# A decoder layer with retrieved experts: 160 instead of 128 tokens take gathered rows, sums run over eight expert tiles, and the spill is spread

## The chip, the cores and the metric

The kernel runs on one core of one Trainium2 chip. A core has a matrix engine (TensorE, here PE), three engines for elementwise work (VectorE or DVE, ScalarE or ACT, GpSimd or POOL), a queue engine (SyncE, SP) and 16 DMA engines that move data between the chip's memory (HBM), the 128-partition working memory (SBUF) and back. PE writes into the accumulators (PSUM). The metric is device time in microseconds (us); lower is better. A time is the median of several executions; one execution is recorded by the hardware profiler.

## The reference

One inference step of one decoder layer, in float32, for 512 prompt tokens and 8 sample tokens (520 together, 2048 wide). Two attention branches are gated, multiplied by `w_out` and added to the input; this gives `h`. Then follows a mixer with retrieved experts (PEER). Of 16384 experts, each token takes 128: 8 heads choose 16 each by product keys. Cut to what matters:

```
hn = rmsnorm(h, norm2_w)                        # 520 x 2048
q = (hn @ wq) per head, in two halves
s = q . subkeys                                 # 8 heads x 2 halves x 128 keys
half_s, half_i = top_k(s, 16)
best_s, best_c = top_k(sums of pairs, 16)       # 16 of 256 candidates per head
experts = i1 * 128 + i2                         # 128 expert numbers per token
gates = softmax(best_s)
act = gelu(hn . u[experts])                     # 128 dot products of 2048 per token
y = h + sum over experts of gates * act * v[experts]
```

`u` and `v` have 16384 rows of 2048 numbers each.

## The kernel before

**Two ways for the experts.** The first `ND` = 392 tokens ("dense") are computed with all 16384 experts: PE multiplies every u row with every dense token, in 128 tiles of 128 experts; the result goes through gelu, is multiplied by a gate that is zero for experts not chosen, and PE multiplies this by all v rows. The last `NS` = 128 tokens ("gathered", one per partition) fetch only their chosen rows: an indirect DMA on POOL's queue brings, for one choice, one row of u or v for each of 128 tokens (128 x 2048 floats, 1 MB).

**Matmuls.** Every float32 weight is split into two parts, `wh` (rounded, ScalarE, L297) and `wl` (the rest, DVE, L299), and every product is three matmuls: wh by yh, wh by yl, wl by yh. `terms` (L331) issues them all on L336; a matmul has 128 columns of weights and as many moving columns as there are tokens. Weights are streamed in the order of `_plan`, 1 MB at a time, in two halves of 1024 columns; `wh` and `wl` have `WB` = 3 buffers of one half each. `terms` counts its columns and calls `tick` after every 16 x 260 of them.

**Stages.**
1. Projection and attention (78 tiles of `win`, matmuls of 260 columns, two per weight tile for the 520 tokens), then the branch products and `w_out`, also 260 and 260.
2. `wq` products, one per head (`q_product`): 392 and 128 columns.
3. u tiles 0 to 69 (`spill_u`): 48 matmuls of 392 columns, gelu, and the result goes out to HBM (`act_d`, issued by POOL). Under these tiles the routing runs: `halves_top` and `best_all` are generators, `tick` makes one step of one of them. `best_all` goes through the five token tiles of `TILES` (tile 0 holds the gathered tokens): top-16 searches on DVE, and for each half of the keys an equality mask on DVE (L1043), a product with the indices on POOL (L1045, 128 x 2048) and a sum on DVE (L1048). For tile 0 the expert numbers and gates go to `eg`. Then `build_g` makes the gates of the dense tokens as a matrix in HBM (`g_d`): for each four tokens DVE builds two masks (eA L1097, Bt L1099), POOL and ScalarE scale them (L1101, L1103, L1104), and PE multiplies them (L1080, 8 matmuls of 128 columns).
4. Experts, from about 2249 us: 32 groups of `GRP` = 4 expert tiles. `c_of` fetches a spilled result (L1232), or computes a u tile from tile 70 on, multiplies it by the gates (L1218) and splits it (L1220, L1221). `v_group` multiplies 4 tiles by v, 16 output chunks, and DVE adds each pair of chunks to `acc` (L1263).
5. `gathered` runs beside stage 4, as one more generator: 128 times a u row is fetched (L1155) and its dot product with `hn` taken on DVE (L1185, the row buffer is overwritten), then gelu and gates, then 128 v rows, each scaled and added to a sum on DVE (L1197). A row is due every `PACE` = 3.1 ticks; there are three row buffers. Before the last group the rest is drained, PE transposes the sum, and it is added to `acc`.

**Order.** PE's and SP's instructions run in the order in which the program writes them; from stage 4 on POOL's do too. The order of the others is set by a planner.

## Time and profile before

| | |
|---|---|
| median of 3 runs | 3904.21 us (3903.19 to 3906.29) |
| the profiled execution | 3891.22 us |
| its span | 3889.5 us |
| PE busy | 3812.2 us (98%), 25080 matmuls |
| PE weight loads (PEld) | 3779.9 us (97%) |
| DVE busy | 2753.0 us (71%) |
| ACT busy | 1436.4 us (37%) |
| POOL busy | 930.5 us (24%) |
| HBM read and written | 836.48 and 150.95 MB, 254 GB/s over the span |

An engine is busy while an instruction of it runs; matmuls overlap, so a busy PE is not PE at its full pace. The page of the profile divides the span into 40 slices and gives the busy share of each in tenths. In the views by line, `L299` is line 299, `wl<-wr,wh` names output and inputs, `x744` the number of instructions. A wait is put down to the instruction that ended it.

### The profile page before, as it was taken

The numbers are of one execution on the slowest core, as the hardware profiler recorded it, in microseconds if no ns is written. First come the engines' busy times: TensorE is split into PE (matmuls) and PEld (weight loads), VectorE is DVE, ScalarE is ACT, GpSimd is POOL, SyncE is SP. The second block draws the span as 40 slices with busy tenths as digits, with TensorE's granted clock in tenths as the row PEclk, the third lists the DMA queues.
The fourth block names the chain that finished last, engine by engine and source line by source line (L and its number), as shares of the span: only waits on it lengthen the run. The fifth ranks groups of instructions, "written<-read, shape, count | busy, mean of one in ns | idle before, by whom it ended". The sixth has DMA issues, their size and how long they took to land.

```text
span 3889.5 us, 61269 instructions
## 1 busy us (share of the span) xinstructions
PE 3812.2 (98%) x25080; PEld 3779.9 (97%) x25080; DVE 2753.0 (71%) x3925; ACT 1436.4 (37%) x2032; POOL 930.5 (24%) x944
## 2 busy tenths in 40 slices
PE   8999999999999999989999999999999999999999
PEld 8999999999999999989999999999999999999999
DVE  5444333778654357898666579999988888888864
ACT  5655444222322322323777532222222323232232
POOL 2111111223210000133666322222222222222200
PEclk9999999999999999999999999999999999999999
DMA  4233334667656333545544579898888889888853
GB/s 164 103 113 137 141 133 183 222 242 260 228 202 236 141 132 116 191 162 197 199 187 184 201 297 336 319 332 318 333 329 330 318 329 337 331 312 304 331 209 131
DMA packets 140761, 901.37 MB, mean 232 GB/s; under 512 B 20096, under 2 KB 21088, under 8 KB 56512
## 3 DMA queue, kind: packets, MB, share of 16 engines
q1 hardware_dynamic: 59296, 489.74, 33.5%
q0 software_dynamic: 66064, 380.27, 26.4%
q10 hardware_dynamic: 15120, 27.43, 2.2%
q8 instruction: 198, 3.24, 0.3%
q14 instruction: 83, 0.68, 0.1%
HBM read 836.48 MB, written 150.95 MB: 254 GB/s over the span
## 4 chain that ended last, share of the span: by engine, by line
PE 84%; DVE 8%; issue 4%; DMA 2%; ACT 1%; POOL 0%; ACTq 0%; POOLq 0%; DVEq 0%
PE mm L336 71%; PE vv L336 8%; DVE wl L299 3%; PE gq L1080 2%; DVE gb L1185 1%; DMA k<-q_d 1%; PE sc L976 0%; ACT wh L297 0%; DMA wr<-in_win 0%; PE a L510 0%; DVE acc L1263 0%; PE a L517 0%; DVE s1b L1048 0%; PE a L523 0%; DVE c L1221 0%
## 5 line engine op out<-in xcount | busy, mean ns | idle before, releaser
L297 ACT ACTIVATE wh<-wr 128x1024 fp32r<-128x1024 f32 x744 | 787.4, 1059 | 1840.3 <-PE mm L336 1454.3
L299 DVE TENSOR_TENSOR wl<-wr,wh 128x1024 fp32r<-128x1024 f32 x744 | 948.3, 1279 | 335.8 <-ACT wh L297 334.0
L336 PE MATMUL mm<-HH,wl 128*128 128x392 f32 x2176 | 755.1, 347 | 15.3 <-DVE wl L299 15.3
L336 PE MATMUL mm<-HH,wh 128*128 128x392 f32 x2176 | 759.1, 349 | 2.1 <-ACT wh L297 1.2
L336 PE MATMUL mm<-HL,wh 128*128 128x392 f32 x2176 | 756.0, 347 | 0.0
L336 PE MATMUL mm<-c,wh 128*128 128x392 f32 x2316 | 608.5, 343 | 3.9 <-DVE c L1221 3.9
L336 PE MATMUL mm<-S,wh 128*128 128x260 f32 x3048 | 589.0, 285 | 8.2 <-ACT S L380 8.2
L336 PE MATMUL mm<-S,wl 128*128 128x260 f32 x2664 | 545.0, 286 | 5.3 <-DVE wl L299 5.3
L336 PEld LDWEIGHTS mm<-S,wh 128*128 128x128 f32 x3048 | 460.2, 190 | 10.4 <-ACT S L380 8.2
L336 PEld LDWEIGHTS mm<-c,wh 128*128 128x128 f32 x2316 | 426.1, 189 | 6.9 <-DVE c L1221 6.1
L336 PEld LDWEIGHTS mm<-HH,wl 128*128 128x128 f32 x2176 | 412.2, 189 | 19.3 <-DVE wl L299 18.6
L336 PEld LDWEIGHTS mm<-S,wl 128*128 128x128 f32 x2664 | 414.5, 190 | 8.8 <-DVE wl L299 5.7
L336 PEld LDWEIGHTS mm<-HH,wh 128*128 128x128 f32 x2176 | 411.5, 189 | 4.0 <-ACT wh L297 1.5
L336 PEld LDWEIGHTS mm<-HL,wh 128*128 128x128 f32 x2176 | 411.6, 189 | 0.9
L336 PE MATMUL mm<-c,wl 128*128 128x392 f32 x1158 | 396.0, 342 | 1.4 <-DVE wl L299 1.4
L336 PE MATMUL mm<-S1a,wh 128*128 128x260 f32 x1520 | 311.0, 286 | 4.2 <-DVE S1a L381 4.1
L336 PE MATMUL mm<-S1b,wh 128*128 128x260 f32 x1520 | 312.2, 287 | 2.1 <-DVE S1b L381 2.1
L336 PE MATMUL vv<-c,wh 128*128 128x392 f32 x1108 | 293.0, 344 | 8.7 <-DVE c L1221 5.5
L1197 DVE SCALAR_TENSOR_TENSOR hb<-gb,dots,hb 128x2048 f32<-128x2048 f32 x127 | 298.1, 2347 | 4.4 <-DMA gb<-in_vn,idx 4.3
L1185 DVE SCALAR_TENSOR_TENSOR gb<-gb,hb 128x2048 f32<-128x2048 f32 x128 | 292.6, 2286 | 3.1 <-DMA gb<-in_un,idx 3.1
L1155 POOL DMA_INDIRECT gb<-in_vn,idx x128 | 158.7, 1240 | 462.5 <-DVE hb L1197 397.3
L336 PEld LDWEIGHTS mm<-S1a,wh 128*128 128x128 f32 x1520 | 235.0, 189 | 6.2 <-DVE S1a L381 5.1
(317 smaller groups left out, 5584.8 us busy)
## 6 DMA issues: line engine op xcount, KB each, us to landing
wr<-in_uT SPq DMA_DIRECT2D x128, 1024.0 KB, 4.9
wr<-in_v SPq DMA_DIRECT2D x128, 1024.0 KB, 7.3
wr<-in_win SPq DMA_DIRECT2D x78, 1024.0 KB, 4.8
g_d<-stg POOLq DMA_DIRECT2D x14, 1792.0 KB, 6.9
ga<-g_d POOLq DMA_DIRECT2D x32, 784.0 KB, 10.8
wr<-in_wout SPq DMA_DIRECT2D x16, 1024.0 KB, 4.8
out_s<-in_c SPq DMA_DIRECT2D x16, 1020.0 KB, 7.3
act_d<-t POOLq DMA_DIRECT2D x70, 196.0 KB, 2.6
```

What stands on the lines that cost most here:

```text
L297: A.activation(h, r, AF.Copy)
L299: V.tensor_tensor(l, r, h, op=OP.subtract)
L336: PE.matmul(ps, u, y[lo >= ND][:, lo % ND:hi - lo + lo % ND] if isinstance(y, tuple) else y[:, lo:hi], start=(begin and i == 0 and a == 0) ...
L1080: PE.matmul(ps[:, t], Bt[:, t], AA[:, t, x], start=x == 0, stop=x == 1)
L1155: G_.indirect_dma_start(out=g, out_offset=None, in_=src, in_offset=bass.IndirectOffsetOnAxis(ap=idx[:, j:j + 1], axis=0))
L1185: V.scalar_tensor_tensor(g, g, 1.0, hn, op0=OP.mult, op1=OP.mult, accum_out=dots[:, j:j + 1])
L1197: V.scalar_tensor_tensor(sums, g, coef[:, j:j + 1], sums, op0=OP.mult, op1=OP.add)
```

## The change

- Dense tokens: 360 instead of 392; gathered: 160 instead of 128. All dense matmuls have 360 columns; `wq` and `w_out` products have 360 and 160 (`w_out` had 260 and 260). The 160 gathered tokens come in two sets: 128 tokens with 128 rows each of u and v as before, and 32 tokens whose 128 choices are spread over four groups of 32 partitions (`RB` = 4), so that 32 fetches each of u and v do.
- `gathered` starts as soon as tile 0 of the routing is done, not in stage 4, and has a clock of its own in `tick`. Its pace in ticks depends on the stage: 4.0 in the rest of the routing, 3.5 in `build_g`, then 2.3 for u rows and 2.9 for v rows. From then on POOL's instructions run in written order.
- The dot products of u rows: in the routing all on POOL (product) and ScalarE (sum), in `build_g` all on DVE, in stage 4 every second one on POOL and ScalarE.
- Groups have 8 expert tiles (16 groups): one weight tile of v holds 8 x 256 columns for two output chunks, and `acc` gets half as many additions. Of every group 3 tiles are computed in place (positions 0, 3, 6) and 5 come from the spill: 80 are spilled instead of 70.
- Gathered tokens have their own part of the sum (`accg`, kept in HBM as `h_d`) and go out on their own. Their `hn` is made early by `hn_rows`, in the `wq` stage.
- `build_g` has 90 steps instead of 98, with three sets of masks instead of two, its gate products two steps behind instead of one, and 1.5 ticks per step instead of 1.33. Spill stores are issued three ticks later (`post`). Copies of cache rows are issued every 7 ticks instead of 9. Buffers are cut differently, so that they fit.

The diff, cut to its core:

```diff
-ND, NS = 392, 128
+ND, NS = 360, 160
+NA_, NB_, RB = 128, 32, 4
 TT, NTT = 128, 5
-TILES = [(ND, NS)] + [(i * (ND // 4), ND // 4) for i in range(4)]
-GC, NGC = 28, 14
-KA = 12
+TILES = [(ND + NB_, NA_), (ND, NB_)] + [(i * (ND // 3), ND // 3) for i in range(3)]
+GC, NGC = 24, 15
+KA = 11
 NEXP = 128
-NSPILL = 70
-GRP = 4
+GRP = 8
+GL = 4
+INLINE = {g * GRP + i for g in range(NEXP // GRP) for i in (0, 3, 6)}
+SPILLED = [i for i in range(NEXP) if i not in INLINE]
+NSPILL = len(SPILLED)
 TICK = 16
 NACT = 3
-COPY_EVERY = 9
+COPY_EVERY = 7
 WB = 3
 MANUAL = ('PE', 'SP')
 HALF = 44
-NCB = 6
+NCB = 10
 NGB = 3
-PACE = 3.1
-PRE = 2
-LEAD = 3
+PACES = {'routing': 4.0, 'gates': 3.5, 'u': 2.3, 'v': 2.9}
+LEAD = 2
+LAG = 2
...
-    p += [("uT", i) for i in range(NSPILL)]
+    p += [("uT", i) for i in SPILLED]
     for g in range(NEXP // GRP):
-        p += [("uT", i) for i in range(g * GRP + (g > 0), min(NEXP, g * GRP + GRP + 1)) if i >= NSPILL]
-        p += [("v", (g, q)) for q in range(4)]
+        p += [("uT", i) for i in range(g * GRP + (g > 0), min(NEXP, g * GRP + GRP + 1)) if i in INLINE]
+        p += [("v", (g, q)) for q in range(8)]
...
+    posts = deque()
+
+    def post(f, lag=3):
+        posts.append((clock["n"] + lag, f))
...
+        while posts and posts[0][0] <= clock["n"]:
+            posts.popleft()[1]()
+        if pace and clock["n"] >= pace["due"]:
+            pace["due"] += next(pace["gen"], 1e9)
...
+    def cut2(ps):
+        return [(ps[:, 0, :ND], 0, ND), (ps[:, 1, :NS], ND, T)]
+
     for c in range(KC):
         w = stream(("wout", c))
         if c < 4:
-            S_.dma_start(acc[:, c * 4:c * 4 + 4, :], I["xT"][:, c * 4:c * 4 + 4, :])
+            S_.dma_start(acc[:, c * 4:c * 4 + 4, :], I["xT"][:, c * 4:c * 4 + 4, :ND])
+            S_.dma_start(accg[:, c * 4:c * 4 + 4, :], I["xT"][:, c * 4:c * 4 + 4, ND:])
         ps = psum_mm()
-        dot3(ps, w, (mH, mL))
-        V.tensor_tensor(v2(acc[:, c]), v2(acc[:, c]), ps[:, :, :TH], op=OP.add)
+        dot3(cut2(ps), w, (mH, mL))
         w2 = cst[:, C_N2 + c:C_N2 + c + 1]
-        A.activation(HHt[:, c], acc[:, c, :ND], AF.Copy, scale=w2)
-        A.activation(HGt[:, c], acc[:, c, ND:], AF.Copy, scale=w2)
-        if c == 0:
-            A.activation(ssq, acc[:, c], AF.Square)
-        else:
-            s = tmp0()
-            A.activation(s, acc[:, c], AF.Square)
+        s = tmp0() if c else ssq
+        for a, h, b, n in ((acc, HHt, 0, ND), (accg, HGt, 1, NS)):
+            V.tensor_tensor(a[:, c], a[:, c], ps[:, b, :n], op=OP.add)
+            A.activation(h[:, c], a[:, c], AF.Copy, scale=w2)
+            A.activation(s[:, b * ND:b * ND + n], a[:, c], AF.Square)
...
+        n, act = nu, u_tile(SPILLED[nu])
+        post(lambda: G_.dma_start(act_d[n], act))
...
+                cell["stage"] = "routing"
+                perm.enter_context(tc.manual_schedule(engines={mybir.EngineType.PE, mybir.EngineType.SP, mybir.EngineType.Pool}))
+                pace.update(gen=gathered(), due=clock["n"] + 2)
                 yield
...
+        cell["stage"] = "gates"
+        eAs = cp.tile([P, 3, 4, P], BF16, name="eA", tag="S1x")
+        Bts = cp.tile([P, 2, 4, P], F32R, name="Bt", tag="S1y")
+        Btx = tp.tile([P, 4, P], F32R, name="t0", bufs=2)
+        AH = [gp.tile([P, 4, P], F32R, name=f"AH{x}") for x in range(3)]
+        AL = [gp.tile([P, 4, P], F32R, name=f"AL{x}") for x in range(2)] + [tp.tile([P, 4, P], F32R, name="t0", bufs=2)]
...
-            if n:
+            yield
+            if n >= LAG:
                 products(*todo.popleft())
-            yield
-            if n % 3 == 2:
+            if n % 2:
                 yield
-        products(*todo.popleft())
-
+        while todo:
+            yield
+            products(*todo.popleft())
+        for _ in range(4):
+            yield
...
+    def hn_rows():
+        yield
+        for c in range(0, KC, 4):
+            hd = k1.tile([P, 4, NS], F32, name="hd", bufs=2)
+            V.tensor_tensor(hd, HGt.bitcast(F32)[:, c:c + 4], HLGt.bitcast(F32)[:, c:c + 4], op=OP.add)
+            V.tensor_tensor(hd, hd, rstd_[:, ND:].unsqueeze(1).to_broadcast([P, 4, NS]), op=OP.mult)
+            yield
+            for lo, n in ((NB_, NA_), (0, NB_)):
+                ps = sc_p.tile([P, 512], F32, name="sc")
+                for i in range(4):
+                    PE.transpose(ps[:n, i * P:(i + 1) * P], hd[:, i, lo:lo + n], ident)
+                dst = hb[:n, c * P:(c + 4) * P] if lo else tmp0()[:n, :512]
+                A.activation(dst, ps[:n], AF.Copy)
+                if not lo:
+                    G_.dma_start(hn_d[:, c * P:(c + 4) * P], dst)
+            yield
+
...
+        homes = ((slp, "S3g"), (cp, "S0g"), (slp, "S2g"))
+        cell["row"] = 0
+
+        def buf():
+            pool, tag = homes[cell["row"] % 3]
+            cell["row"] += 1
+            return pool.tile([P, D], F32, name=f"row{tag}", tag=tag)
+
+        def rows(side, idx, S, use):
             fetched = deque()
+            src = I["un" if side == "u" else "vn"]
+            for j in range(S + 2):
+                if j < S:
+                    g = buf()
                     G_.indirect_dma_start(out=g, out_offset=None, in_=src,
                                           in_offset=bass.IndirectOffsetOnAxis(ap=idx[:, j:j + 1], axis=0))
                     fetched.append((j, g))
+                if len(fetched) == 3 or j >= S:
                     use(*fetched.popleft())
+                yield PACES[cell['stage'] if cell['stage'] in PACES else side]
+
+        for e, S, n, c0 in ((eg, P, NA_, NB_), (egb, P // RB, NB_, 0)):
+            idx = hp.tile([P, P], I32, name="idx")[:, :S]
+            dots = hp.tile([P, P], F32, name="dots")[:, :S]
+            V.tensor_copy(idx, e[:, 0])
+            hn = hb
+            if S < P:
+                hn = hp.tile([P, D], F32, name="hb")
+                for r in range(RB):
+                    G_.dma_start(hn[r * NB_:(r + 1) * NB_], hn_d)
+
+            def dot(j, g):
+                if cell["stage"] == "routing" or cell["stage"] == "experts" and j % 2:
+                    G_.tensor_tensor(g, g, hn, op=OP.mult)
+                    A.activation(g, g, AF.Copy, accum_out=dots[:, j:j + 1])
+                else:
+                    V.scalar_tensor_tensor(g, g, 1.0, hn, op0=OP.mult, op1=OP.mult, accum_out=dots[:, j:j + 1])
+
+            yield from rows("u", idx, S, dot)
+            A.activation(dots, dots, AF.Gelu)
+            V.tensor_tensor(dots, dots, e[:, 1], op=OP.mult)
+            sums = hp.tile([P, D], F32, name="hb")
+
+            def add(j, g):
+                if j == 0:
+                    V.tensor_scalar(sums, g, dots[:, 0:1], None, op0=OP.mult)
+                else:
+                    V.scalar_tensor_tensor(sums, g, dots[:, j:j + 1], sums, op0=OP.mult, op1=OP.add)
+
+            yield from rows("v", idx, S, add)
+            hx = buf()[:, :KC * n].rearrange("p (c t) -> p c t", c=KC)
+            G_.dma_start(hx, h_d[:, :, c0:c0 + n])
+            yield PACES['v']
             for q in range(2):
                 ps = vp.tile([P, 2, 512], F32, name="gt")
                 for c in range(KC // 2):
+                    k = q * 8 + c
+                    PE.transpose(ps[:, c // 4, (c % 4) * P:(c % 4) * P + P], sums[:, k * P:(k + 1) * P], ident)
+                dst = hx[:, q * 8:q * 8 + 8]
+                part = ps.rearrange("p x (c n) -> p (x c) n", c=4)
+                for r in range(P // n):
+                    V.tensor_tensor(dst, dst, part[:, :, r * n:(r + 1) * n], op=OP.add)
+                yield 1
+            G_.dma_start(O["y"][:, :, ND + c0:ND + c0 + n].rearrange("c p t -> p c t"), hx)
...
+        if i in INLINE:
+            c_tile(i, u_tile(i))
+            return
+        n = SPILLED.index(i)
+        while len(acts) < LEAD:
+            load_act()
+        c_tile(i, acts[n])
+        if len(acts) < NSPILL:
+            load_act()
+
+    def load_act():
+        acts.append(tp.tile([P, ND], F32, name="t0", bufs=2))
+        G_.dma_start(acts[-1], act_d[len(acts) - 1])
...
-        for dq in range(4):
-            w = stream(("v", (g, dq)))
-            for d2 in range(2):
-                dc = dq * 4 + d2 * 2
-                wh, wl = w[d2]
+        for dc in range(0, KC, 2):
+            w = stream(("v", (g, dc // 2)))
+            for _ in range(1):
                 nv += 1
                 ps = vp.tile([P, 2, 512], F32, name="vv") if nv % 3 == 0 else psum_mm()
                 todo = []
                 for dl in range(2):
-                    items = []
-                    for t in range(GRP):
-                        c = t * 256 + dl * P
-                        items.append((wh[:, c:c + P], wl[:, c:c + P]) + Cs[g * GRP + t])
+                    items = [pick(w, t * 256 + dl * P) + Cs[g * GRP + t] for t in range(GRP)]
...
-            cell["rush"] = True
-            drain()
+            for _ in pace["gen"]:
+                pass
...
```

## Rows read from the trace of the kernel before

**Rows 1.** The page: busy tenths of DVE in 40 equal slices of the span.
```profile
DVE  5444333778654357898666579999988888888864
```

**Rows 2.** The chain that ended last: start us, us, what.
```profile
377.09 9.60 PE mm L336 x80
...
1422.12 4.59 PE mm L336 x32
...
2286.23 8.56 PE mm L336 x48
...
2326.88 8.67 PE mm L336 x48
```

**Rows 3.** Windows: busy time (instructions) of each engine, PEclk, DMA share, GB/s.
```profile
1620.00:1826.00 206.00, 190.15 (x1012) 186.16 (x1010) 203.83 (x511) 68.01 (x82) 73.79 (x42) 0.96 0.47 173
1826.00:2179.00 353.00, 352.30 (x2267) 352.26 (x2268) 233.53 (x292) 259.19 (x483) 229.66 (x239) 1.00 0.51 191
2249.00:2860.00 611.00, 589.11 (x3230) 581.09 (x3229) 551.93 (x587) 176.05 (x200) 162.82 (x178) 0.99 0.88 326
...
3000.00:3700.00 700.00, 700.00 (x3911) 699.37 (x3910) 606.93 (x500) 210.51 (x246) 166.83 (x135) 1.00 0.86 323
2249.00:3889.00 1640.00, 1611.62 (x8937) 1601.18 (x8935) 1387.02 (x1313) 478.87 (x552) 375.87 (x356) 1.00 0.82 307
```

**Rows 4.** Groups by form: busy us, mean ns of one, idle before, releasers.
```profile
L299 DVE TENSOR_TENSOR wl<-wr,wh 128x1024 fp32r<-128x1024 f32 x744 | 948.3, 1279 | 335.8 <-ACT wh L297 334.0
L297 ACT ACTIVATE wh<-wr 128x1024 fp32r<-128x1024 f32 x744 | 787.4, 1059 | 1840.3 <-PE mm L336 1454.3 <-PE vv L336 207.5 <-DMA wr<-in_v 29.2
...
L1197 DVE SCALAR_TENSOR_TENSOR hb<-gb,dots,hb 128x2048 f32<-128x2048 f32 x127 | 298.1, 2347 | 4.4 <-DMA gb<-in_vn,idx 4.3
...
L1185 DVE SCALAR_TENSOR_TENSOR gb<-gb,hb 128x2048 f32<-128x2048 f32 x128 | 292.6, 2286 | 3.1 <-DMA gb<-in_un,idx 3.1
...
L1263 DVE TENSOR_TENSOR acc<-acc,mm 128x784 f32<-128x784 f32 x171 | 165.9, 970 | 87.4 <-PE mm L336 86.6
...
L1218 DVE TENSOR_TENSOR t<-t,ga 128x392 f32<-128x392 f32 x128 | 70.7, 562 | 4.6 <-DMA t<-act_d 1.9 <-ACT t L932 1.8 <-DMA ga<-g_d 0.9
```

**Rows 5.** Timeline of DVE and POOL in routing: start us, us, what, idle before.
```profile
1652.49 4.24 DVE L1035 SCALAR_TENSOR_TENSOR s1b<-s1b 128x128 f32<-128x128 f32 x1
...
1722.70 0.28 DVE L1035 SCALAR_TENSOR_TENSOR s1b<-s1b 98x128 f32<-98x128 f32 x1
1722.90 1.22 DVE L299 TENSOR_TENSOR wl<-wr,wh 128x1024 fp32r<-128x1024 f32 x1
...
1742.37 4.58 POOL L1045 TENSOR_TENSOR s1a<-s1a,s1b 98x2048 f32<-98x2048 f32 x1 [7.65 <-DVE s1a L1043]
...
1816.28 4.69 DVE L299 TENSOR_TENSOR wl<-wr,wh 128x1024 fp32r<-128x1024 f32 x1
```

**Rows 6.** Timeline of DVE and of POOL in the gate stage.
```profile
1953.53 0.69 DVE L1097 TENSOR_TENSOR eA<-cst,i1T 128x512 bf16<-128x512 f32 x1 [0.93 <-POOL AA L1104]
1954.14 0.69 DVE L1099 TENSOR_TENSOR Bt<-cst,i2T 128x512 fp32r<-128x512 f32 x1
...
1956.12 0.69 DVE L1097 TENSOR_TENSOR eA<-cst,i1T 128x512 bf16<-128x512 f32 x1 [0.81 <-POOL AA L1104]
...
1954.37 0.72 POOL L1101 TENSOR_TENSOR AA<-eA,gH 128x128 fp32r<-128x128 bf16 x1 [0.87 <-DVE eA L1097]
1955.05 1.03 POOL L1104 TENSOR_TENSOR AA<-eA,gL 128x512 fp32r<-128x512 bf16 x1
```

**Rows 7.** Timeline of PE at one gate step.
```profile
1854.31 1.00 PE L1080 MATMUL gq<-AA,Bt 128*128 128x128 f32 x8
1855.14 0.40 PE L336 MATMUL mm<-HH,wh 128*128 128x392 f32 x1
```

**Rows 8.** Timeline of PE at six small matmuls of the attention.
```profile
858.62 0.85 PE L788 MATMUL a<-db,ones 32*128 32x32 f32 x6
```

**Rows 9.** The row fetches, line 1155: time from issue to landing.
```profile
DMA to landing us min/median/max: 5.2/8.0/14.8
```

More of the change, by code (lines that the diff above doesn't have):

```diff
@@ L186, in _program @@
     V.memset(ones, 1.0)
-    onesR = cp.tile([P, P], F32R, name="onesR")
-    V.tensor_copy(onesR, ones)
     epst = cp.tile([P, 1], F32, name="epst")
@@ L193, in _program, with joined @@
     osm = cp.tile([P, 12, DB], F32, name="osm")
-    eg = cp.tile([P, 2, P], F32, name="eg")
     def slot(tag, dt, chunks=KC):
         return cp.tile([P, chunks, T], dt, name=tag, tag=tag)
+    def joined(*tiles):
+        at = [t[:, i] for t in tiles for i in range(t.shape[1])]
+        return lambda k: at[k]
     def halves(dt):
-        a, b = slot("S1a", dt, 8), slot("S1b", dt, 8)
-        return lambda k: (a if k < 8 else b)[:, k % 8]
+        return joined(*(slot(tag, dt, n) for tag, n in (("S1a", 6), ("S1x", 2), ("S1b", 6), ("S1y", 2))))
     def parts(dt):
-        a, b = slot("S0", dt, KA), slot("S0g", dt, KC - KA)
-        return lambda k: a[:, k] if k < KA else b[:, k - KA]
+        return joined(slot("S0", dt, KA), slot("S0g", dt, KC - KA))
     def whole(t):
@@ L226, in _program @@
     act_d = dp.tile([NSPILL, P, ND], F32, name="act_d")
+    h_d = dp.tile([P, KC, NS], F32, name="h_d")
+    hn_d = dp.tile([NB_, D], F32, name="hn_d")
     g_d = dp.tile([NGC, P, NK, GC], F32, name="g_d")
     clock = {"n": 0}
+    pace = {}
     first, active, queue = deque(), deque(), deque()
@@ L256, in drain @@
     def drain(all_=True):
-        while first:
-            first.popleft()[1]()
-        while all_ and (active or queue):
-            step()
+        while first or posts or all_ and (active or queue):
+            if first or posts:
+                (first or posts).popleft()[1]()
+            else:
+                step()
     copies = []
@@ L431, in start_attention @@
         sp = at.enter_context(tc.tile_pool(name="sp", bufs=1))
+        onesR = sp.tile([P, P], F32R, name="onesR")
+        V.tensor_copy(onesR, ones)
         tab = sp.tile([P, 512], F32, name="tab")
@@ L1010, in cand, with by_slot @@
             return c
+        def by_slot(t, rows):
+            t0, m = TILES[t]
+            ps = sc_p.tile([P, 512], F32, name="sc")
+            for x in range(3):
+                PE.transpose(ps[:, x * P:x * P + m], rows[:, x], ident[:m, :m])
+            ts = slice(t0, t0 + m)
+            V.tensor_copy(i1T[:, ts], ps[:, 0:m])
+            V.tensor_copy(i2T[:, ts], ps[:, P:P + m])
+            A.activation(gH[:, ts], ps[:, 2 * P:2 * P + m], AF.Copy)
+            V.tensor_tensor(gL[:, ts], ps[:, 2 * P:2 * P + m], gH[:, ts], op=OP.subtract)
         nxt = cand(0)
+        left = None
         yield
@@ L1020, in best_all @@
                 yield
+                if h == 4 and left:
+                    by_slot(*left)
+                    left = None
             if t + 1 < NTT:
@@ L1113, in _program @@
+    queue.append(hn_rows())
     for h in range(PH):
@@ L1177, in gathered @@
-        for _ in range(4):
-            yield
-        hn = cpl.tile([P, D], F32, name="hb")
-        yield from turn(lambda c: hd[:, c],
-                        lambda q, ps: A.activation(hn[:, q * 1024:(q + 1) * 1024].rearrange("p (x n) -> p x n", x=2),
-                                                   ps, AF.Copy))
-        def dot(j, g):
-            V.scalar_tensor_tensor(g, g, 1.0, hn, op0=OP.mult, op1=OP.mult, accum_out=dots[:, j:j + 1])
-        yield from rows(I["un"], dot)
-        coef = dots
@@ L1261, in v_group, with begin @@
                         terms(out, items[-1:], begin=False)
-                dst = acc[:, dc:dc + 2, :ND]
+                dst = acc[:, dc:dc + 2]
                 V.tensor_tensor(dst, dst, ps[:, :, :ND], op=OP.add)
                 if g == NGRP - 1:
-                    (G_ if dc < KC - 2 else S_).dma_start(O["y"][dc:dc + 2].rearrange("c p t -> p c t"), acc[:, dc:dc + 2])
-    routed_at = None
-    while nu < NSPILL:
-        spill_u()
-        if routed_at is not None:
-            for i in range(PRE * (nu - routed_at - 1), min(GRP, PRE * (nu - routed_at))):
-                c_of(i)
-        elif not active and not queue:
-            routed_at = nu
-            rt.close()
-            pr.close()
-            start_experts()
-            load_g(0)
-    if routed_at is None:
-        drain()
+                    (G_ if dc < KC - 2 else S_).dma_start(O["y"][dc:dc + 2, :, :ND].rearrange("c p t -> p c t"), acc[:, dc:dc + 2])
+    def begin():
         rt.close()
@@ L1283, in _program @@
         start_experts()
-    perm.enter_context(tc.manual_schedule(engines={mybir.EngineType.PE, mybir.EngineType.SP, mybir.EngineType.Pool}))
-    queue.append(gathered())
+        load_g(0)
+        load_g(1)
+        cell["stage"] = "experts"
+    while nu < NSPILL:
+        spill_u()
+        if cell.get("stage") != "experts" and not active and not queue:
+            begin()
+    if cell.get("stage") != "experts":
+        drain()
+        begin()
+    drain(False)
     c_of(0)
```

173 lines of the change are left out of this document (70 added, 103 removed).

## Prediction

> **What bounds the kernel now.** I read the page first. By its table TensorE (PE) is busy for 98% of 3889.5 us and its weight loads for 97%; VectorE (DVE) has 71%, but its tenths rise to 7 to 9 in the routing slices and in the last 40% [rows 1]. Matmuls overlap, so busy is no proof of full pace, and next I took the pace from the chain that ended last: 80 matmuls of 260 columns take 9.60 us (120.0 ns each), 48 of 392 columns 8.56 us (178.3 ns), 48 in the v sums 8.67 us (180.6 ns) [rows 2]. With these, the stages of the windows view can be weighed [rows 3].
>
> - Projection, attention and w_out up to 1389 us: PE runs, and nothing here but w_out changes.
> - Routing, 1620 to 1826: 1012 matmuls, all but some twelve transposes u matmuls of 178.3 ns, are 178 us of 206. PE lost 28 us and DVE was busy for 203.8 of 206: DVE sets this stage.
> - Gate matrix (`build_g`), 1826 to 2179: PE is full.
> - Experts, 2249 to the end: 128 v tiles of 8.67 and 58 u tiles of 8.56 us are 1606 of 1640 us; 31 us are lost, nearly all before 2860, where DVE is 90% busy. From 3000 to 3700 DVE is 87% busy and PE loses nothing.
>
> So PE bounds most of it, with DVE close behind, and saturated in routing. The reader should see in [rows 5] why: while POOL multiplies 128x2048 (4.6 us), a DVE instruction with two inputs in SBUF that takes 0.28 or 1.22 us alone lasts 4 us or more, until POOL ends. Instructions of DVE with one input or with PSUM go on meanwhile. Each of the ten POOL products of routing holds up one DVE instruction (the first and the last of the ten are shown), together by 39 us: 3.9 us each. In the gate stage they take turns too: eA, Bt, then POOL's two products, and the next eA starts as POOL ends, 2.59 us per step of four tokens [rows 6].
>
> **The change: what PE gains.** From 260 to 392 columns a matmul grows by 58.3 ns, 0.442 ns per column. 32 columns fewer are 14.1 ns, on 6144 u and 6144 v matmuls: -174 us. Eight fewer gate steps at 0.83 us [rows 7]: -7.
>
> What PE pays: 160 columns beside 360. In the wq products a pair of 392 and 128 columns takes 4.59/16 = 287 ns [rows 2], so 128 columns cost 108.6 ns, far above their share. 32 columns behind a 128-column weight load cost about 0.11 us as well: six in 0.85 us, less the 0.27 us that the last one's latency adds [rows 8]. So a matmul seems to cost at least its weight load, and 160 columns cost between 108.6 ns (the floor) and 135.7 (in proportion); I take the floor, which the 32-column row speaks for. The new pair is 164.2 + 108.6 = 272.8 ns. For w_out it replaces two of 120.0, on 768 pairs: +25 (up to +46). For wq it replaces 287, on 384 pairs: -5 (up to +5). Together +20, up to +51. [...]
>
> 32 more transposes at some 0.1 us: +3. Sum for PE: 3889.5 - 174 - 7 + 20 + 3 = 3731.5. Without the old losses of 28 and 31 us it would be 3672.5.
>
> **What the other engines get.** A tick is 4160 columns of `terms`: at 360 columns 11.56 matmuls, 1.90 us (1.92 in the v sums). Each tick steps one routing generator, so stages are counted in ticks, and rows in ticks over the pace.
>
> - *Routing after tile 0*: 4 tiles of 19 steps and 5 more, 81 ticks, 154 us of PE. At pace 4.0 about 20 rows are fetched and 18 dots go to POOL and ScalarE. DVE's own work was 203.8 - 39 = 165 us for five tiles, so 131 for four; the eight old POOL products hold it for 31, and the new ones, which have the same shape, for 18 x 3.9 = 70. 232 against 154: **+78**. ScalarE's pass per dot is hidden: it was busy 68 of 206 us.
> - *Gate stage*: 90 steps at 1.5 ticks and some 8 more: 143 ticks, 271 us, with 90 x 0.83 us of gate matmuls 346. In turns, DVE and POOL need 90 x 2.59 = 233 us, 34 u tiles of two splits (2.35 us) 81, and 41 dots at 2.37 us (2.29 and reading the sum, 0.08) [rows 4] 97: 411. **+65**. (Before: 98 x 2.59 + 31 x 2.35 = 327 of 353, so it fitted.)
> - *Experts, u rows*: about 67 rows are left of the first set and 32 of the second, 50 pairs of one DVE and one POOL dot, at 2 x 2.3 ticks: 8.8 us of PE a pair. DVE's base per tick, over 731 ticks: 352 splits at 1.18 (1.22, a little overlapped), 128 c tiles at 2 x 0.52, 48 u results at 0.52 (562 ns, scaled), 128 additions into acc at 0.89 (half of them gone; 970 ns, scaled) [rows 4]: 687 us, 0.94 per tick. A pair has 4.3 + 2.4 + 3.9 = 10.6 us: +1.8 each, **+90**.
> - *Experts, v rows*: 160 rows at 2.9 ticks, 5.55 us each. DVE needs 2.73 + 2.35 = 5.08, 92%, above the 90% at which PE lost 4% and the 87% at which it lost nothing. A v tile's second half also has less time now: all eight expert tiles of one output chunk use both halves, so the buffer comes free at three quarters of the tile before and is wanted at one quarter: 4 us instead of 8.6. ScalarE's 1.06 and DVE's 1.22 [rows 4, 5] fit, but not behind a 2.35 us row: 0.6 us late. Rows fill 42% of DVE: 128 x 0.42 x 0.6 = 32 at worst; I take 20.
> - *The end*: about 723 ticks of rows stand against 716 before the last group is issued; the rest is rushed there, and PE's transposes wait for the last rows: +5 (up to 15).
> - *POOL's queue* is now in written order from routing tile 0 on: gathers, products, spill stores and loads. It hides while it is no fuller than DVE: per pair 4.6 + 2 x 0.94 + about 0.6 of loads is 7.1 of 10.6 us. A late product there delays the spill store and then the `t1` buffer of u_tile.
> - Costed at nothing: denser copies (SP; DMA is half idle before the experts [rows 3]), the moved onesR, later spill stores, the h_d and hn_d transfers (small, long before use).
>
> New waits: 78 + 65 + 90 + 20 + 5 = 258. Span 3672.5 + 258 = 3930.5; the profiled execution's time lies 1.7 above its span, and the median of the runs 13 above the profiled one: **3945 us**, 1.0% slower. The measurement can tell some 0.2%, 8 us, from no change.
>
> With b for the time that one POOL dot holds DVE, the waits are 68b - 7 (68 dots: 18 and 50). They eat PE's gain of 217 at **b = 3.3 us**; the rows say 3.9. The Trainium skill, GPSIMD Engine Reference (Performance versus the Vector engine; Engine selection), advises against POOL for such products, as a 2048-column one takes 4.50 us against 2.29; held that long the waits would be 299, 41 us more. The row agrees in length (4.6), but DVE does some work with one input meanwhile.
>
> **The rivals.**
> - *DVE keeps up (faster).* If DVE's order lets instructions with one input or PSUM (additions into acc, u results, the top-16 searches) run during POOL's products, or few two-input instructions meet them, b falls below 3.3. With none of it, the old 28 and 31 us of waits and 10 in the gate stage: 3672.5 + 69 = 3742, in the runs 3756. For it: DVE has about 13% free in the last stage; POOL was busy only 24%. Against: ten of ten products met one. Chance 0.32, spread from 3756 to 3896.
> - *It cancels.* b near 3.3: 3904. Chance 0.07.
> - *Transfers bind as well (still slower).* In the v rows, weights (1.05 MB per 7.9 us), spills and gates (27 GB/s) and rows (1.05 MB per 5.55 us) ask for 349 GB/s, and the experts stage carried 326 to 328 at a DMA share of 0.88 [rows 3]. Were that the limit, 903 us of v rows grow by 58; with w_out's upper bound, +31: 4034. Against: the share was not 1. Chance 0.13.
> - *Row supply binds.* Three buffers, landing in 8.0 us [rows 9]: POOL rows take about 16.6 us round, DVE rows 11.8, so 9.5 per pair, hidden under 10.6. Landing in 11 us would give 11.5, +45. It is in the range.
>
> **How the numbers follow.** The forecast (3900 to 4010 on its own) has 0.48; a little of it lies within 8 us of 3904. Faster 0.33, same 0.07, slower 0.60. The range is 3770 to 4045: it takes in nearly all of the faster case and the transfer case, and leaves out 0.1 at each end.
>
> **What would show it.** Right: u matmuls at 164 ns and w_out pairs near 273; in routing after tile 0 and in the experts' u rows, splits (wl) and rows of 3 to 5 us beside POOL products, DVE near 100%, PE with gaps released by wl; gate stage over 390 us; a clean, faster v stretch. Wrong: DVE instructions of normal length beside POOL's dots, a gate stage near 346 us, or PE waiting on weights from DMA instead.

## The result: 4082.1 us, 4.6% slower than before

The changed kernel took 4082.11 us (median of four runs, 4078.69 to 4085.39); the kernel before took 3903.97 us beside it. The ratio is 1.0455 (95% interval 1.0437 to 1.0473). The forecast was 3945 us, range 3770 to 4045: the direction was right, the loss more than four times as large, and the time lies above the range. The profiled execution has a span of 4076.9 us. Beside the experiments, on other chips, the kernel before took 3893.9 to 3897.2 us; ratios there are to that. Executions of one variant lie up to 0.4% to either side of their median, so a single execution tells no difference under some 15 us; the experiments that stand without a ratio are single executions.

The page of the changed kernel, engines and tenths, answers to [rows 1]:

```profile
PE 3757.5 (92%) x25045; PEld 3697.6 (91%) x25045; DVE 2923.2 (72%) x3767; ACT 1571.9 (39%) x2160; POOL 1466.7 (36%) x1103
...
PE   8999999999999999976799987778999999998899
...
DVE  5444334776752367999999977777888888878784
...
PEclk9999999999999999997899998899999999999899
```

PE now has holes in two places: in the rest of the routing (slices 18 to 20), where DVE is at 9, and in the experts' u rows (slices 24 to 28), where DVE is only at 7. The second is what I had not foreseen. The granted clock falls in both.

The windows view by stages (columns as in [rows 3]): rest of the routing, gate stage, u rows of the 128 tokens, their v rows, u rows of the 32 tokens, their v rows and the end. (Below, the "first" u and v rows are those of the 128 tokens.)

```profile
1731.00:1986.00 255.00, 179.69 (x957) 176.12 (x956) 233.44 (x334) 95.84 (x116) 163.02 (x79) 0.83 0.50 179
1986.00:2375.00 389.00, 359.39 (x2279) 350.98 (x2278) 384.55 (x350) 267.30 (x450) 305.99 (x269) 0.96 0.72 268
2375.00:2835.00 460.00, 364.02 (x2003) 353.01 (x2002) 348.89 (x249) 173.93 (x197) 277.71 (x141) 0.89 0.75 280
2835.00:3573.00 738.00, 710.27 (x4233) 704.97 (x4232) 619.84 (x523) 229.55 (x268) 253.65 (x182) 0.99 0.88 334
3573.00:3812.00 239.00, 211.22 (x1197) 205.89 (x1196) 192.71 (x144) 92.59 (x108) 139.23 (x71) 0.95 0.76 284
3812.00:4077.00 265.00, 241.91 (x1401) 238.05 (x1399) 181.36 (x165) 70.92 (x81) 63.62 (x53) 0.94 0.72 264
```

The chain (start us, us, what) gives the pace of an undisturbed 360-column matmul, 39.66/240 = 165.3 ns (164.2 were forecast); above it, among the chain's longest links, stand 15 of POOL's products of rows, new in this kernel, and four loads of spilled results, of which the chain of before has one (7.48 us). One of each, and then the undisturbed matmuls:

```profile
2465.90 8.12 DMA t<-act_d
2481.55 4.50 POOL rowS2g L1254
...
2911.12 39.66 PE mm L352 x240
```

**What each stage loses** is its length, less its 360-column matmuls at 165.3 ns and its gate products and transposes at 104 ns ([rows 7]: 0.83 us for eight). In the third window: 460 - 2003 x 0.1653 = 129. All comparisons below use this measure (stage borders from the trace, to 0.1 us):

| us lost | forecast | changed | all dots on DVE (e1) | POOL's dots left out (e2) | product, no sum (e3) | three fills (e15) |
|---|---|---|---|---|---|---|
| u tiles under tile 0 | 0 | 5 | 4 | 5 | 5 | 4 |
| rest of the routing | 78 | 97 | 63 | 21 | 103 | 51 |
| gate stage | 65 | 56 | 49 | 50 | 50 | 55 |
| u rows (both sets) | 90 | 171 | 59 | 60 | 145 | 64 |
| v rows and end | 25 | 73 | 56 | 61 | 70 | 68 |
| sum | 258 | 402 | 230 | 196 | 373 | 242 |
| time of the runs | 3945 | 4082 | 3905 | 3865 | 4046 | 3911 |

The rest, 4076.9 - 402 = 3674.7 us, is PE's own work; 3672.5 were forecast.

A held DVE in the u rows (timelines of DVE and POOL, as in [rows 5]):

```profile
2580.46 4.81 DVE L1295 TENSOR_TENSOR t<-t,ga 128x360 f32<-128x360 f32 x1 [0.57 <-ACT t L959]
...
2593.48 5.23 DVE L1298 TENSOR_TENSOR c8S1x<-t,c8S1x 128x360 fp32r<-128x360 f32 x1 [0.57 <-ACT c8S1x L1297]
...
2580.28 4.59 POOL L1254 TENSOR_TENSOR rowS3g<-rowS3g,hb 128x2048 f32<-128x2048 f32 x1
2589.87 2.33 POOL L1235 DMA_INDIRECT rowS3g<-in_un,idx  x1 [5.00 <-ACT rowS3g L1255]
...
2593.74 4.57 POOL L1254 TENSOR_TENSOR rowS2g<-rowS2g,hb 128x2048 f32<-128x2048 f32 x1
```

The multiplication by the gates and the split of a c tile, 0.53 us each otherwise, last until POOL's product ends. Between the products a fetch stands for 5.0 us waiting for ScalarE's sum, and what follows it in POOL's order stands too. The groups by line in the same stretch (2375 to 2835) show what that makes on average, against 1221 and 2286 ns with all dots on DVE:

```profile
L315 DVE TENSOR_TENSOR wl<-wr,wh 128x1024 fp32r<-128x1024 f32 x83 | 177.8, 2148 | 65.6 <-ACT wh L313 64.1 <-issue 1.5
L1257 DVE SCALAR_TENSOR_TENSOR rowS2g<-rowS2g,hb 128x2048 f32<-128x2048 f32 x11 | 38.0, 3451 | 9.3 <-DMA rowS2g<-in_un,idx 9.3
...
L1295 DVE TENSOR_TENSOR t<-t,ga 128x360 f32<-128x360 f32 x27 | 20.4, 785 | 4.2 <-DMA t<-act_d 2.5 <-ACT t L959 1.7
```

Splits 83 x 0.93 = 77 us, the 35 dots 27, the c tiles 12: 116 us on 35 products, 3.3 us each. And yet DVE idles for 66 us in front of the splits. What PE waits for in that stretch (total, times, longest):

```profile
PE vv L352 <- DVE wl L315: 18.6, 8, 3.7
PE mm L352 <- DVE wl L315: 17.1, 9, 3.4
PE mm L352 <- ACT c8S1b L1297: 15.4, 2, 8.4
PE vv L352 <- ACT c8S1b L1297: 10.6, 1, 10.6
```

Not a full DVE, but single late pieces: splits by 2 to 4 us, c tiles by 8 to 11.

### The profile page after: what moved, and what is told of

Its sections match the earlier page's. It is cut to its first block, busy times and chain, and to the rows that moved or that the text cites. A ratio compares the mean times of both kernels' runs of the same rounds, so it can differ in the third digit from the quotient of the medians.

```text
span 4076.9 us, 61597 instructions
## 1 busy us (share of the span) xinstructions
PE 3757.5 (92%) x25045; PEld 3697.6 (91%) x25045; DVE 2923.2 (72%) x3767; ACT 1571.9 (39%) x2160; POOL 1466.7 (36%) x1103
## 5 line engine op out<-in xcount | busy, mean ns | idle before, releaser
L352 PE MATMUL mm<-HH,wl 128*128 128x360 f32 x2176 | 740.7, 340 | 46.6 <-DVE wl L315 46.3
L352 PE MATMUL mm<-HH,wh 128*128 128x360 f32 x2176 | 738.5, 339 | 42.3 <-DVE t L958 38.2
L352 PE MATMUL mm<-HL,wh 128*128 128x360 f32 x2176 | 737.6, 339 | 0.0
L352 PE MATMUL mm<-S,wh 128*128 128x260 f32 (+2 forms) x2698 | 540.1, 288 | 7.9 <-ACT S L396 7.9
L352 PE MATMUL mm<-S,wl 128*128 128x260 f32 (+2 forms) x2474 | 513.2, 289 | 5.1 <-DVE wl L315 5.1
L352 PE MATMUL mm<-c8S1b,wh 128*128 128x360 f32 x1120 | 285.6, 336 | 24.4 <-ACT c8S1b L1297 21.7
L352 PE MATMUL mm<-cb,wh 128*128 128x360 f32 x1072 | 271.0, 334 | 11.0 <-ACT cb L1297 9.0
L352 PE MATMUL mm<-S1b,wh 128*128 128x260 f32 (+1 forms) x1140 | 239.3, 292 | 0.9 <-DVE S1b L397 0.9
L352 PE MATMUL mm<-S1a,wh 128*128 128x260 f32 (+1 forms) x1140 | 238.0, 290 | 1.8 <-DVE S1a L397 1.7
L352 PEld LDWEIGHTS mm<-c8S1b,wh 128*128 128x128 f32 x1120 | 204.9, 194 | 27.6 <-ACT c8S1b L1297 23.1
```

The lines of the kernel that those rows point to most:

```text
L352: PE.matmul(ps, u, y[lo >= ND][:, lo % ND:hi - lo + lo % ND] if isinstance(y, tuple) else y[:, lo:hi], start=(begin and i == 0 and a == 0) ...
```

## The experiments

**Where the dots are taken.** e1 gives them all to DVE; e2 leaves POOL's out (`dots` is cleared first, as in e3, e13, e15 and e16); e3 keeps POOL's product without ScalarE's sum.

```diff
# e1
-                if cell["stage"] == "routing" or cell["stage"] == "experts" and j % 2:
+                if False:
# e2: both lines out; e3: the second line out
                     G_.tensor_tensor(g, g, hn, op=OP.mult)
                     A.activation(g, g, AF.Copy, accum_out=dots[:, j:j + 1])
```

> All dot products of u rows go to DVE; POOL keeps the gathers and the loads, ScalarE sums no rows. The changed kernel loses, beyond its matmuls at 165.3 ns, about 100 us in routing after tile 0, 55 in the gate stage, 130 and 49 in the two stretches of u rows and 46 and 20 in those of v rows. If POOL's products cost by holding DVE (the hold), routing loses about 50 and the u rows about 30 together: 3850 to 3920 us. If POOL's queue in written order costs more (product, ScalarE's sum, next gather, and the loads of spilled results and gates behind them), the chain gets shorter too, since a gather then waits for 2.4 us on DVE instead of 6.7 on two engines, but the loads still wait in it: 3900 to 3950. If the supply of rows or the transfers bind, little changes: above 4000 us.

3904.6 us, ratio 1.0027 (1.0013 to 1.0042): 177 us less than the changed kernel (some 167 by the ratios, as the chips differ), where the bounds of both theories overlap. The offloaded dots alone turn a tie into 4.6%. In routing the splits fall from 3.13 to 1.48 us on average, in the u rows to 1.22:

```profile
L315 DVE TENSOR_TENSOR wl<-wr,wh 128x1024 fp32r<-128x1024 f32 x82 | 99.2, 1221 | 26.7 <-ACT wh L313 25.1 <-issue 1.4
```

> Leaves out the dot products that POOL and ScalarE took (all in routing, every second one in the experts): the rows are fetched and not used, their sums stay zero. Hold, or POOL's queue: routing loses about 10 to 30 us instead of 100, u rows 20 to 60 instead of 179, so 3820 to 3880 us in all. Supply or transfers: all rows still come, so above 3980 us.

3865.4 us, as expected. But the u rows lose 60 us as with e1, though DVE is busy for 62% there instead of 81%: this part of the loss comes neither from POOL's dots nor from how busy DVE is. Windows of the first u rows, e1 and then e2 (42 or 43 us are lost in each):

```profile
2328.90:2702.10 373.20, 342.28 (x1999) 337.17 (x1998) 303.46 (x318) 107.77 (x129) 126.92 (x106) 0.96 0.93 349
...
2284.20:2648.30 364.10, 337.44 (x1950) 330.87 (x1949) 225.40 (x244) 105.32 (x125) 105.34 (x103) 0.96 0.92 352
```

> Keeps every product on POOL and leaves out ScalarE's sum of it, so that the next gather into that buffer waits for POOL alone; the sums of these rows stay zero. Hold: DVE meets as many products as before and the time falls by less than 40 us, 4040 to 4080. POOL's queue: the gathers waited for ScalarE's sum for 127 us of the 484 us of the first u rows, and that goes: u rows lose 80 to 110 us less, 3960 to 4000 us.

4046.2 us. Of 402 us lost, 29 go; the wait for the sum is not the main part. Splits in the u rows get longer still, as rows come faster (2371 to 2802):

```profile
L315 DVE TENSOR_TENSOR wl<-wr,wh 128x1024 fp32r<-128x1024 f32 x80 | 202.3, 2545 | 38.4 <-ACT wh L313 38.4
```

**The hold or POOL's time.** e8 puts half of the dots on POOL in the kernel before, and nothing else. e10 multiplies by a number (one input), e13 also drops the sum; e15 and e16 fill the buffer three or two times, without a sum.

```diff
# e8, kernel before
+            if j % 2:
+                G_.tensor_tensor(g, g, hn, op=OP.mult)
+                A.activation(g, g, AF.Copy, accum_out=dots[:, j:j + 1])
+            else:
                 V.scalar_tensor_tensor(g, g, 1.0, hn, op0=OP.mult, op1=OP.mult, accum_out=dots[:, j:j + 1])
# e10, e13
-                    G_.tensor_tensor(g, g, hn, op=OP.mult)
+                    G_.tensor_scalar(g, g, 1.5, None, op0=OP.mult)
# e15 (e16: range(2))
+                    for _ in range(3):
+                        G_.memset(g, 1.0)
```

> The kernel before with one part of the change: every second dot product of u rows on POOL, its sum on ScalarE. A pair of rows is 12.8 us of PE there. Hold: DVE's own work in that time (2249 to 2860: 552 us of 611, less some 105 dots of 2.4 us, is 50%) is 6.4 us, the dot that it keeps 2.4 and the hold 3.9, 12.7 us, so DVE is full and PE loses 10 to 40 us: 3905 to 3935. If only POOL's chain counts (product 4.6, sum 2.1, two gathers 2.0, is 8.7 us), it fits and the time stays within 10 us of 3894 or is less.

4023.7 us, ratio 1.0335 (1.0318 to 1.0352): 128 us more than the kernel before. By POOL's chain alone the time would have stayed within 10 us, so the hold was the right theory of the two, but its size was three times my 10 to 40 (the run does not part it from the wait for ScalarE's sum). Window and split group from 2249 to 2860 (589 us of PE and 552 of DVE in [rows 3], splits of 1.22 us):

```profile
2249.00:2860.00 611.00, 530.68 (x2785) 516.55 (x2784) 543.42 (x426) 226.06 (x254) 343.59 (x196) 0.94 0.76 279
```

```profile
L299 DVE TENSOR_TENSOR wl<-wr,wh 128x1024 fp32r<-128x1024 f32 x116 | 277.5, 2392 | 10.3 <-ACT wh L297 10.3
```

The splits alone grow by 136 us, the c tiles by 29, on some 41 products: 4.0 us each, the 3.9 of [rows 5].

> The changed kernel, but POOL multiplies these rows by a number (one input in SBUF, 128x2048) instead of by hn; ScalarE's sum stays, the dots of these rows are other ones. If DVE is held only where POOL reads two inputs: the splits beside POOL take 1.2 us, routing loses 50 to 65 instead of 97, the u rows 60 to 110 instead of 171: 3950 to 4000 us. If any POOL instruction of that size holds DVE: splits of 3 to 6 us as before and 4060 us or more. If POOL's instruction gets much shorter, its chain does too, and the u rows lose about 60 as without POOL's dots: 3900 to 3920.

4086.8 us. POOL's instruction got longer, and the splits did not get back to 1.2 us (2.3 in routing, where the products of the routing itself hold them too, 1.8 in the u rows):

```profile
L1254 POOL TENSOR_SCALAR rowS0g<-rowS0g 128x2048 f32<-128x2048 f32 x12 | 65.3, 5442 | 2.8 <-DMA rowS0g<-in_un,idx 2.6
```

```profile
L315 DVE TENSOR_TENSOR wl<-wr,wh 128x1024 fp32r<-128x1024 f32 x82 | 144.1, 1762 | 77.2 <-ACT wh L313 77.0
```

The run does not take the hold away, and so it decides nothing. But its timelines show how long one input holds:

```profile
2418.39 5.43 POOL L1254 TENSOR_SCALAR rowS3g<-rowS3g 128x2048 f32<-128x2048 f32 x1
2420.08 3.09 DVE L315 TENSOR_TENSOR wl<-wr,wh 128x1024 fp32r<-128x1024 f32 x1 [2.79 <-ACT wh L313]
...
2442.82 5.42 POOL L1254 TENSOR_SCALAR rowS0g<-rowS0g 128x2048 f32<-128x2048 f32 x1
2446.26 2.39 DVE L1257 SCALAR_TENSOR_TENSOR rowS2g<-rowS2g,hb 128x2048 f32<-128x2048 f32 x1 [4.68 <-DMA rowS2g<-in_un,idx]
```

The split ends 1.22 us, its own length, after a point 3.6 us into POOL's 5.4; the dot, which begins 3.4 us into the next product, takes hardly more than its 2.29 us. The others go the same way: a two-input instruction that begins earlier is held until some 3.55 us into a one-input product. With two inputs it is some 4.5 us, POOL's end, for all 39 splits and dots that began beside a product of rows in the changed kernel (three of them waited longer still).

> The changed kernel with POOL multiplying its rows by a number (one input, 5.4 us) and without ScalarE's sum of them (these sums stay zero). The u rows lose 171 us in the changed kernel, 145 without the sum, 187 with one input, 60 without POOL's dots. If the hold and the chain each suffice to slow them, taking both away brings 60 to 90 and the routing 40 to 60: 3900 to 3950 us. If the hold alone counts, it is as with one input: above 4030. If POOL's busy time alone counts (5.4 us and two gathers a pair), the u rows lose 130 or more: above 3980.

4040.0 us, u rows 136 lost, splits of 2.1 us: undecided for the same reason.

> The changed kernel, in which POOL fills its rows' buffers with a constant three times instead of multiplying them, and ScalarE's sum is left out (these sums stay zero); with the product and without the sum it is e3_no_act_sum, 4046 us (u rows lose 145 us, routing 103, splits 2.5 us on average in the first u rows). The fill's length is read from the trace. If the hold counts: splits near 1.22 us, the u rows lose 50 to 75 and the routing 20 to 45, 3860 to 3910 us, even where three fills take longer than the product. If POOL's time in its written order counts: as much loss as with the product for the same length of POOL's work, 4000 us or more.

> The same with two fills. If the hold counts: as with three, within 15 us. If POOL's time counts: the loss of the u rows shrinks with the length of POOL's work per row, between that of e2_no_pool_dots (60, nothing on POOL) and that with three fills.

3910.6 and 3882.7 us. Groups of three fills in the first u rows (2300 to 2680):

```profile
L315 DVE TENSOR_TENSOR wl<-wr,wh 128x1024 fp32r<-128x1024 f32 x83 | 101.1, 1224 | 65.4 <-ACT wh L313 65.4
```

```profile
L1256 POOL MEMSET rowS2g<- 128x2048 f32 x33 | 60.0, 1817 | 1.3
```

Three fills take 5.45 us in the place of a product of 4.6, and the splits beside them last 1.22; none is held. The u rows lose 64 us, not the 145 of e3. That settles it for the u rows: what costs is the hold, not POOL's time. In routing both count: 103 us with the product, 51 with three fills (20 to 45 were expected), 39 with two, 21 with nothing; e16 lies 28 us below e15, not within 15. The Trainium skill, SBUF — State Buffer ("Who interferes with whom"), says that a DVE instruction with two SBUF inputs contends with a GpSimd instruction that reads SBUF, not with one that only writes it; the fills agree (1.22 us beside them, 2.55 beside products).

**What is lost without POOL's dots.** e7 leaves out all gathered rows.

```diff
-                pace.update(gen=gathered(), due=clock["n"] + 2)
+                pace.update(gen=iter(()), due=clock["n"] + 2)
```

> The changed kernel without gathered rows: nothing is fetched, and the 160 gathered tokens get no expert output and are not written. What is left is PE's own work and the losses that do not come from rows. PE's sum of the prediction without old losses was 3672.5; with 165.3 ns for 360 columns (measured) it is 3686. If the losses come with the rows: 3690 to 3720 us. If routing (20 us in e2_no_pool_dots) and the gate stage (50 us in all versions so far) lose by themselves: 3740 to 3770.

3707.4 us: the first case. Windows of the rest of the routing and of the gate stage:

```profile
1730.00:1890.00 160.00, 147.72 (x849) 145.35 (x850) 149.80 (x319) 56.06 (x73) 53.36 (x39) 0.96 0.39 139
1890.00:2260.00 370.00, 369.38 (x2473) 368.75 (x2472) 263.58 (x292) 286.09 (x462) 220.02 (x235) 1.00 0.51 189
```

Routing loses 20 us by itself, the gate stage 5, all else 10. So by the spans (3705.6 here) the rows cost 371 us in the changed kernel and still 196 with all dots on DVE, against PE's gain of 217.

e5 fetches half rows (DVE's time as before), e12 and e14 change `'u': 2.3` in `PACES` to 3.1 and 2.6. e5 stands on e1; e6, on e1 too, interleaves the v tile; e12 and e14 stand on e6.

```diff
# e5
-                    G_.indirect_dma_start(out=g, out_offset=None, in_=src,
+                    G_.indirect_dma_start(out=g[:, :D // 2], out_offset=None, in_=src.rearrange("e (x d) -> (e x) d", x=2),
# e6
                     for out, items in todo:
-                        terms(out, items)
+                        terms(out, items[:4], end=False)
+                    for out, items in todo:
+                        terms(out, items[4:], begin=False)
```

> The version with all dots on DVE (e1_dve_dots, 3904.6 us), but every fetch brings 128 half rows (1024 numbers, 4 KB) instead of whole ones; DVE works as long as before on them (a dot is two instructions over the same half, an add reads the half twice), so the sums of the gathered tokens are other ones. That version still loses 43 and 16 us in the u rows and 32 and 24 in the v rows. If the transfers bind there (DMA share 0.93 in the u rows), the u rows lose 0 to 25 in all and the v rows under 30: 3830 to 3865 us. If DVE, or the waits in POOL's queue, cause them, under 15 us change: 3890 to 3910.

3898.9 us, hardly less, but for two opposite reasons (windows of the first u and v rows):

```profile
2335.00:2716.00 381.00, 333.73 (x1953) 325.04 (x1952) 305.59 (x455) 106.37 (x126) 119.66 (x105) 0.98 0.67 239
2716.00:3414.00 698.00, 696.33 (x4207) 694.55 (x4206) 613.92 (x520) 224.46 (x265) 246.68 (x183) 1.00 0.72 256
```

The v rows lose 11 us in both sets instead of 56: there the transfers bind, and DVE at 88% is no hindrance. The u rows lose 92 instead of 59; DVE waits 64 us for fetched rows, though they are half as large. Bytes are not what makes these late.

> The version with all dots on DVE (e1_dve_dots, 3904.6 us), but a v tile goes through expert tiles 0 to 3 for both output chunks and then through 4 to 7, so that a half of the weights is free after half of the tile again (8 us for the next half instead of 4). The prediction took 20 us for that window (32 at worst); the v rows lose 56 us in this version. If the window causes it, they lose 20 to 35 and the time is 3870 to 3890; if the rows' landing or POOL's blocked queue does, the time stays within 10 us: 3895 to 3915.

3895.1 us, ratio 1.0000 (0.9989 to 1.0011), the best version that computes everything, and no faster than before. The v rows lose 45 instead of 56: the window of the weights is worth some 10 us, half of what the prediction took.

> e6_interleave with a u row every 3.1 ticks in the experts, as in the kernel before, instead of 2.3. If the time that a row takes to come (three buffers, a fetch behind two others) sets the u rows, they lose 10 to 30 us in all instead of 59; about 100 rows then need 80 ticks more, so some 28 rows are rushed before the last group while PE waits, 3 to 5 us each: 3940 to 4000 us. If DVE or the c tiles cause the loss, it stays above 45.

3930.2 us. First u rows, and the last v rows with the end:

```profile
2325.00:2751.00 426.00, 415.62 (x2494) 414.12 (x2493) 345.13 (x366) 135.11 (x163) 125.35 (x111) 0.99 0.88 334
...
3724.00:3928.00 204.00, 110.14 (x657) 109.18 (x655) 123.69 (x91) 29.23 (x32) 50.62 (x42) 0.77 0.64 233
```

At the pace of before the u rows lose 22 us in all instead of 59; the rows that are left over then cost 97 at the end. So the loss hangs on the pace of the rows. That three buffers cannot bring one every 2.3 ticks, 4.4 us, is one reading of it and not shown: in the first u rows of e1 DVE waits 16 us for fetched rows, while POOL's fetches stand 180 of 373 us until DVE has freed a buffer.

> e6_interleave (3895.1 us) with a u row every 2.6 ticks in the experts. At 2.3 the u rows lose 59 us and the end 22, at 3.1 22 and 97. If the first falls faster than the second rises, 3870 to 3890; if they trade one for one, 3890 to 3905.

3916.3 us, 1.0061 (1.0044 to 1.0078): u rows 54, last stretch 44 (22 before). Longer than either case expected: no trade.

**The loads in POOL's queue.** e4 puts both loads on SP; e9, on e6, issues them two ticks later; e11 also changes paces (routing 6.0, v 2.8).

```diff
# e4 (load_g alike)
-        G_.dma_start(acts[-1], act_d[len(acts) - 1])
+        S_.dma_start(acts[-1], act_d[len(acts) - 1])
# e9 (the next gates alike)
-        if len(acts) < NSPILL:
-            load_act()
+        if len(acts) < NSPILL:
+            post(lambda: len(acts) >= min(n + 3, NSPILL) or load_act(), 2)
```

> The loads of spilled results and of gates are issued by SP instead of POOL, nothing else. Hold: under 20 us less, 4060 to 4085. POOL's queue: PE waited for c tiles for 50 us in the first u rows, and there and in the v rows the gathers stood behind loads that waited up to 13 us for their buffers; without that 60 to 110 us less, 3970 to 4020. If SP's own queue then holds back the weights, PE waits for wh and wl after weight loads instead, and the time is as before or longer.

4213.5 us. SP then stands in front of these loads (197 us for gates, 218 in the two largest waits for spilled results), the weights come late, and PE waits 150 us for wh. It says nothing about POOL's queue.

> The version with all dots on DVE and interleaved v tiles (e6_interleave, 3895.1 us; it loses 43 and 16 us in the u rows, 23 and 22 in the v rows), in which a load of a spilled result or of gates is issued two ticks (3.8 us) after the c tile that frees its buffer, so that it waits less for that buffer in POOL's queue with gathers behind it. If these blocked loads cause the losses of the u rows: they lose 20 to 40 in all, the v rows 25 to 40, 3855 to 3880 us. If they don't: within 10 us of 3895; if the loads then come too late, PE waits for c tiles and it is longer.

3904.3 us, 1.0028 (1.0016 to 1.0039). The u rows lose 65 (59 in e6), the v rows 55 (45): the blocked loads are not the cause, or they now come late in turn.

> The version with late loads (e9_late_loads) with a row every 6 ticks instead of 4 in the routing, and every 2.8 instead of 2.9 in the v rows. About 7 of 20 rows leave the routing, where DVE is full (95%) and each costs about 2.4 us: routing loses 40 to 48 instead of 61. If the later stages take them at no price, 10 to 20 us less than with late loads; if the v rows are bound by transfers (0.90 there), they give it back: within 6 us.

3921.9 us, 1.0066 (1.0050 to 1.0083). Routing loses 45 instead of 63, the later stages 25 more, above all the u rows (83 instead of 65). It was expected below e9 or within 6 us of it.

## Why the prediction was right and wrong

**Right.** PE's own time: 3674.7 against 3672.5. Its terms: dense matmuls at 165.3 instead of 164.2 ns (13 us more); the `w_out` pair at 100 us / (742/2) = 269.6 instead of 272.8 ns, at the floor and not in proportion. These two make 10 us more; that the sum is off by only 2 is in part luck:

```profile
1200.00:1300.00 100.00, 100.00 (x742) 100.00 (x741) 1.00 0.55 206
```

The hold, too: 3.3 us of DVE per product in the first u rows here, 4.0 in e8, against 3.9. Routing (97 against 78; DVE was busy for 233 us, 232 were reckoned, but the stage took 255) and the gate stage (56 against 65, DVE at 99%) went by the steps as put. The sign was rightly read: without POOL's dots (e1) there is a tie. Too simple was that DVE's instructions with one input go on beside POOL's products. The searches do, but a shift of 0.21 us (L1071, one input) is held until POOL's product ends:

```profile
1760.83 4.87 DVE L1071 TENSOR_SCALAR s1y<-bc 120x128 uint32<-120x128 uint32 x1
1761.01 4.58 POOL L1254 TENSOR_TENSOR rowS0g<-rowS0g,hb 128x2048 f32<-128x2048 f32 x1
```

**Experts, u rows: the step that failed most, 171 instead of 90.** It set 10.6 us of DVE against 8.8 of PE per pair, as if a full DVE were the limit, and "row supply" of 9.5 us was to hide under it. DVE was busy for 76%. Two losses add up instead. 60 us are there without POOL's dots and fall to 22 at the old pace. The nearest to it is the row-supply rival, priced at 45 at most and kept as a side case. What sets this part stays open: half the bytes and later loads did not help, and DVE hardly waited for rows. The other 111 us come with POOL's dots (26 go with ScalarE's sum, 81 more with the hold): the hold delays single splits and c tiles by 2 to 10 us, which PE's few buffers don't cover, however idle DVE is otherwise.

**Experts, v rows: 73 instead of 25.** The half-tile window is worth 10, not 20. Most of the rest is the rival "transfers bind as well", which reckoned 58 us: with all dots on DVE 56 us are lost, and with half rows 45 of them go. The other 17 of the 73 are not assigned. I set the rival aside because a DMA share of 0.88 is not 1; but at 0.88 PE loses 38 us here in the first v rows.

**Break-even in b.** The formula, 68b - 7, leaves nothing to lose (-7) where POOL's dots hold DVE no longer. In fact 196 us are lost without POOL's dots (21 routing, 50 gates, 60 and 61 rows, 5 else), and POOL's dots add 206: 29 through ScalarE's sum (e3), 131 through the hold (e3 against e15), up to 46 through POOL's time (e15 against e2, with a longer instruction than the product). Even with b = 0 the changed kernel would have gained hardly 1%.

**Costed at nothing: the clock.** Of the 402 us, 281 are idle PE (lengths less busy times in the windows); the other 121 are, for the most part, matmuls at the lower clock: by the trace PE is busy for 190 us at a granted clock of 0.50, where a matmul takes 0.30 us instead of 0.165, and that makes some 85 (an estimate). PE after a wait, and the clock there:

```profile
2502.58 1.28 PE L352 MATMUL mm<-cb,wh 128*128 128x360 f32 x2 [8.69 <-ACT cb L1297]
...
2504.86 0.80 PE L352 MATMUL mm<-c8S1b,wh 128*128 128x360 f32 x2
2505.46 0.50 PE L352 MATMUL mm<-c8S1b,wl 128*128 128x360 f32 x1
...
2508.01 0.49 PE L352 MATMUL mm<-c8S1x,wh 128*128 128x360 f32 x2
```

```profile
2504.00:2507.00 3.00, 3.00 (x12) 3.00 (x11) 1.90 (x2) 1.87 (x4) 2.30 (x3) 0.50 0.21 41
2508.00:2513.00 5.00, 5.00 (x33) 5.00 (x32) 2.47 (x1) 1.02 (x1) 4.98 (x2) 1.00 1.01 379
```

After 8.69 us without a matmul the granted clock is 0.50 (1.2 GHz): three matmuls in 0.90 us instead of 0.50, until about 2507.3. These 4.7 us at little more than half the pace cost some 2 us on top of the wait; in routing the mean clock is 0.83.

Sum: 258 + 5 (tile 0) + 19 (routing) - 9 (gates) + 81 (u) + 48 (v, end) = 402, and with 3674.7 the 4077 us measured.

## What to carry to other kernels

A product moved to another engine is not free because that engine is idle: look for instructions of the busy engine that last as long as the other's, and count delayed pieces on PE's path, not only busy shares. Before spreading fetches over more stages and at a faster pace, ask of each stage what it has spare (DVE's time, the transfers, the round of the buffers); here each row that left one stage was paid for in another. A stage that is nearly full loses more than its wait, since PE's clock falls in the gaps.
